# A fixed instruction order for the first mixer of a two-layer trunk, with two maps' logits on two row halves

## The chip, the cores and the metric

The kernel runs on one core of one Trainium2 chip. A core has five engines with queues of their own: TensorE (PE; its weight loads are listed apart as PEld), VectorE (DVE), ScalarE (ACT), GpSimd (POOL) and SyncE (SP, which only starts transfers). They share the on-chip memory SBUF; PE writes its products to the eight banks of PSUM, from where DVE and ACT fetch them. The metric is the device time of one execution in microseconds (us), the median of several runs.

## The reference

A trunk of two layers works on 512 tokens of 1024 features. In each layer a norm is followed by two mixers that share one output projection, then by sixteen experts of which a token uses two, then by a gated embedding. The change is in layer 0, whose mixers are A (differential attention, four heads) and B (a matrix memory, four heads). Mixer A, shortened:

```python
qa = rope(heads(qa, 8, 64)); ka = rope(heads(ka, 8, 64)); va = heads(va, 4, 128)
for each head n, each block of 128 queries:
    logits[m] = q[2n+m] @ k[2n+m].T / 8        # m = 0, 1: the two maps of a head, 64 features each
    logits[m] = where(key_chunk <= query_chunk, logits[m], -inf)
    probs[m]  = softmax(logits[m])
    out       = (probs[0] - lam * probs[1]) @ v[n]
out = rmsnorm(out, gain) * (1 - lam_init)
```

Mixer B takes q and k of its heads through a causal convolution of width 4 and a SiLU, multiplies decayed products of q and k with the values, normalizes, and gates the result. `concatenate([A, B]) @ w_out` is added to the residual `h`.

## The kernel before

All weights come as one stream of units of [128, 1024]; two units are one transfer of 1 MB on SP's queue. `unit` (L220) splits a unit into two float32r parts whose sum is the weight: ACT writes the upper part (`whi`, L193), DVE the rest (`wlo`, L194). A product of two split operands is three matmuls (`mm3`, L231 to L234). One head's q or k is `proj_f` (L260): one unit, 24 matmuls of 512 columns into one bank of the ring `m`. There are two rings of four PSUM banks, `m` and `w`.

Mixer A starts at L471. `rotated` (L473) projects q and k of a head, and ACT evicts them into `qk` (L477); four transfers on POOL's queue write a copy with the 32-row groups swapped (`sw`, L480); POOL multiplies `sw` with the sines (L481), DVE multiplies `qk` with the cosines (L482) and adds both (L483). Then come the four blocks of 128 queries, and block i sees 128 (i + 1) keys. For each of the two maps, `logits` multiplies 64 rows of q and k (L499: map 0 is on partitions 0 to 63, map 1 on 64 to 127), adds the mask by a product with the identity (L500, bfloat16), and calls `softmax_block`: maximum (L360), its negation (L361), exponential with a sum (L362), reciprocal (L363). L511 to L513 combine both maps, `put_T` turns the block (L369, L370), `pv` multiplies with the values (L383), and `mean_ln` (L330) with L517, L518 scales the result of a head. In it, ACT squares (L333) and splits (L334), DVE makes the lower part (L335), and PE sums both parts over the partitions (L338, L339).

Mixer B follows: `values(vb)` and the gates `og` are 192 matmuls, each head has two projections with `conv_silu` (L289), and `out_proj` (L344) multiplies the results of mixer A, 96 matmuls, and later those of B.

Nothing of this order is binding. The recording layer schedules all instructions of the mixers by priorities and estimated costs, so each engine's queue mixes several heads and stages. Within a queue every engine is in order. A tile of a ring is free again when its last reader is done.

Of the kernel before, what the change touches and what calls it, by code (L numbers as in the profile page):

```python
# [16 lines left out]
S = 512  # L17
DM = 1024
T = 4
# [9 lines left out]
# columns of the constants that follow from the shapes  # L29
# [4 lines left out]
# columns of the small parameters  # L34
# [17 lines left out]
# rooms that the units of a further block take in turn  # L52
# [14 lines left out]
def _layer_units(layer):  # L67
    """Order in which the units of [128, 1024] weights are used."""
    if layer == 0:
# [3 lines left out]
        u += [("T", 5, k) for k in range(4)] + [("T", 6, k) for k in range(4)]  # L73
        for n in range(NH):
            u += [("F", 3, n), ("F", 4, n)]
# [30 lines left out]
def tile_hybrid_trunk(ctx, tc, x, wst, gains, small, lam, rwt, cst, out, stop=None):  # L106
# [49 lines left out]
    def transposed(cx):  # L156
        """Room for transposed rows, in two parts."""
        xtp = cx.enter_context(pool_("xt", 1))
        xt[:] = [xtp.tile([128, KD, S], F32R, name="xt" + i) for i in "hl"]

    def banks(cx, **n):
        """Banks of PSUM for one part of the kernel: "m", and one or more rings for the rest."""
        W.psum = cx.enter_context(pool_("psum", 1, space=bass.MemoryType.PSUM))
        W.banks = n
        W.ring = "w"
# [13 lines left out]
    def load(src, eng=None, pool=None, c=None):  # L179
        """A chunk of two units."""  # L180
# [7 lines left out]
    def split(src, a=None, place=None):  # L188
        """Two parts of a unit."""
# [9 lines left out]
    def ahead(eng=None, pool=None):  # L199
        """Load the next chunk of the stream before its units are asked for."""  # L200
# [35 lines left out]
    def norm_scale(t, xn, r):  # L236
        """1 / sqrt(mean(h^2) + eps) of a tile's tokens; xn is room for the squares."""
# [42 lines left out]
    def values(v):  # L280
        """Values by token, [128, tile, 128] for each head."""
# [19 lines left out]
    def rows_split(r, rows):  # L301
        """Rows of four heads as two exact parts, on partitions 0 and 32."""
# [9 lines left out]
    def log_sigmoid_rows(r4, ps, r0, bias):  # L312
        """log(sigmoid(rows + bias)) at partitions 0 to 3, and a spare row."""
# [9 lines left out]
    def cols_of(c, rows):  # L323
        """Rows [4, 512] as columns [128, tile, head]."""
# [5 lines left out]
    def mean_ln(tmp, src, scale):  # L330
        """log(scale * sum over partitions of src^2 + eps), on every partition."""
# [12 lines left out]
    def out_proj(mix):  # L344
        m = len(mix)
        for nh in range(2):
# [10 lines left out]
    def softmax_block(p, ps, n):  # L357
        """exp(ps - max) and 1 / sum over the n keys of one block of queries."""
        nm = st.tile([128, 4], F32, name="nm", bufs=6)
        nc.vector.reduce_max(nm[:, 0:1], ps[:, :n], axis=AX.X)  # L360
        ts(nm[:, 1:2], nm[:, 0:1], -1.0, None, op0=OP.mult)  # L361
# [49 lines left out]
    banks(ctx, m=4, w=4)  # L411

    def even_mixer():
        with ExitStack() as cx:
# [31 lines left out]
            # gates of the mLSTM  # L446
# [17 lines left out]
            # rows of the results that no block may write  # L464
# [6 lines left out]
            # A  # L471
            mix = []
            def rotated():  # L473
                qk = mp.tile([128, 2, S], F32, name="qk")
                for i in range(2):
                    ps = proj_f(unit("F", 8))
                    act(qk[:, i, :], ps, AF.Copy, scale=0.125 if i == 0 else 1.0)  # L477
                sw = mp.tile([128, 2, S], F32, name="sw", bufs=1)
                for q in range(4):
                    nc.gpsimd.dma_start(out=sw[q * 32:(q + 1) * 32], in_=qk[(q ^ 1) * 32:(q ^ 1) * 32 + 32])  # L480
                nc.gpsimd.tensor_tensor(sw, sw, sinb, op=OP.mult)  # L481
                tt(qk, qk, cosb, op=OP.mult)  # L482
                tt(qk, qk, sw, op=OP.add)  # L483
                return qk

            qkn = rotated()
            for n in range(NH):
                qk = qkn
                if n + 1 < NH:
                    qkn = rotated()  # L490
                wt = mp.tile([128, 4, S], F32, name="wt", bufs=1)

                def logits(i):
                    nk = 128 * (i + 1)
                    pr = []
                    for m in range(2):
# [906 lines left out]
```

## Time and profile before

| what | value |
|---|---|
| three runs | 1488.6, 1483.21, 1483.45 us; median 1483.45 us |
| profiled execution, first to last instruction | 1487.2 us |
| PE busy in it | 1396.7 us (94%) |
| DVE busy | 1118.5 us (75%) |
| ACT busy | 916.9 us (62%) |
| POOL busy | 136.9 us (9%) |
| mean granted clock of TensorE | 0.974 |

The profiled execution is another one than the three runs, and of its own time the table has the span alone; the launch around the span is not part of it. Matmuls overlap in their pipeline, so a busy PE says only that there is something in it. How fast a stretch goes is read from the starts of its matmuls. The granted clock is 1.00 at full speed and 0.50 at half.

### The profile page before, as it was taken

The numbers are of one execution on the slowest core, as the hardware profiler recorded it, in microseconds if no ns is written. First come the engines' busy times: TensorE is split into PE (matmuls) and PEld (weight loads), VectorE is DVE, ScalarE is ACT, GpSimd is POOL, SyncE is SP. The second block draws the span as 40 slices with busy tenths as digits, with TensorE's granted clock in tenths as the row PEclk, the third lists the DMA queues.
The fourth block names the chain that finished last, engine by engine and source line by source line (L and its number), as shares of the span: only waits on it lengthen the run. The fifth ranks groups of instructions, "written<-read, shape, count | busy, mean of one in ns | idle before, by whom it ended". The sixth has DMA issues, their size and how long they took to land. (4 is left out here: it accounts for less than half of the span.)

```text
span 1487.2 us, 18591 instructions
## 1 busy us (share of the span) xinstructions
PE 1396.7 (94%) x6728; PEld 1096.0 (74%) x6728; DVE 1118.5 (75%) x1633; ACT 916.9 (62%) x1424; POOL 136.9 (9%) x143
## 2 busy tenths in 40 slices
PE   6999999969987999999999999999969989999996
PEld 4765677748865888877787887878648868888875
DVE  5466568679976999987776556575589979999875
ACT  4334566348865888885655536452448868888855
POOL 2121012010000000003011000100010000000030
PEclk9998999989999999999999999999989999999998
DMA  9331123478985999915431111111478989999261
GB/s 346 134 95 43 57 85 119 186 265 322 412 353 210 410 404 410 396 74 221 142 113 37 50 57 58 58 49 37 198 265 325 420 338 404 404 407 387 93 252 57
DMA packets 54652, 323.28 MB, mean 217 GB/s; under 512 B 6481, under 2 KB 6897, under 8 KB 23569
## 3 DMA queue, kind: packets, MB, share of 16 engines
q1 hardware_dynamic: 36576, 250.38, 43.7%
q0 software_dynamic: 12640, 52.16, 9.4%
q10 hardware_dynamic: 5328, 19.40, 3.3%
q8 instruction: 57, 0.93, 0.3%
q14 instruction: 51, 0.41, 0.1%
HBM read 292.55 MB, written 27.26 MB: 215 GB/s over the span
## 5 line engine op out<-in xcount | busy, mean ns | idle before, releaser
L194 DVE TENSOR_TENSOR wlo<-raw,whi 128x1024 fp32r<-128x1024 f32 x478 | 565.8, 1223 | 92.6 <-ACT whi L193 91.1
L193 ACT CAST whi<-raw 128x1024 fp32r<-128x1024 f32 x478 | 492.3, 1055 | 166.3 <-PE m L234 94.8
L232 PE MATMUL m<-whi,eh 128*128 128x512 f32 x528 | 213.4, 404 | 1.6 <-ACT whi L193 1.6
L233 PE MATMUL m<-wlo,eh 128*128 128x512 f32 x528 | 210.6, 399 | 1.5 <-DVE wlo L194 1.4
L234 PE MATMUL m<-whi,el 128*128 128x512 f32 x528 | 210.0, 398 | 0.0
L233 PE MATMUL m<-xtl,whi 128*128 128x512 f32 (+1 forms) x368 | 142.5, 388 | 0.8 <-DVE xtl L257 0.8
L234 PE MATMUL m<-xth,wlo 128*128 128x512 f32 (+1 forms) x368 | 142.9, 389 | 0.0
L232 PE MATMUL m<-xth,whi 128*128 128x512 f32 (+1 forms) x368 | 141.7, 386 | 0.5 <-ACT xth L256 0.5
L232 PE MATMUL m<-whi,xth 128*128 128x512 f32 x288 | 118.3, 412 | 2.7 <-ACT xth L256 1.2
L233 PEld LDWEIGHTS m<-wlo,eh 128*128 128x128 f32 x528 | 100.3, 190 | 25.6 <-DVE wlo L194 3.4
L232 PEld LDWEIGHTS m<-whi,eh 128*128 128x128 f32 x528 | 100.4, 190 | 25.1 <-ACT whi L193 2.1
L234 PE MATMUL m<-whi,xtl 128*128 128x512 f32 x288 | 117.1, 408 | 1.6 <-DVE xtl L194 1.1
L234 PEld LDWEIGHTS m<-whi,el 128*128 128x128 f32 x528 | 99.9, 189 | 24.3 <-DVE el L842 0.8
L233 PE MATMUL m<-wlo,xth 128*128 128x512 f32 x288 | 116.8, 406 | 0.5 <-DVE wlo L194 0.5
L232 PE MATMUL m<-whi,hh 128*128 128x512 f32 x256 | 102.9, 407 | 0.0
L233 PE MATMUL m<-wlo,hh 128*128 128x512 f32 x256 | 101.8, 399 | 0.3 <-DVE wlo L194 0.3
L234 PE MATMUL m<-whi,hl 128*128 128x512 f32 x256 | 102.0, 399 | 0.0
L233 PEld LDWEIGHTS m<-xtl,whi 128*128 128x128 f32 x368 | 70.6, 192 | 13.0 <-DVE xtl L257 1.0
L232 PEld LDWEIGHTS m<-xth,whi 128*128 128x128 f32 x368 | 70.5, 192 | 12.7 <-ACT xth L256 0.9
L234 PEld LDWEIGHTS m<-xth,wlo 128*128 128x128 f32 x368 | 70.5, 192 | 11.7 <-issue 0.7
L849 POOL DMA_INDIRECT xg<-xrow,toki x32 | 34.1, 1066 | 488.6 <-PE w L839 432.9
L841 ACT CAST eh<-w 128x512 fp32r<-128x512 f32 x82 | 46.9, 590 | 39.1 <-PE w L839 37.8
(427 smaller groups left out, 2307.0 us busy)
## 6 DMA issues: line engine op xcount, KB each, us to landing
raw<-in_wst_dram SPq DMA_DIRECT2D x226, 1024.0 KB, 7.8
raw<-in_wst_dram POOLq DMA_DIRECT2D x14, 1024.0 KB, 7.5
yrow<-y ACTq DMA_DIRECT2D x17, 512.0 KB, 8.6
yrow<-gbc ACTq DMA_DIRECT2D x14, 512.0 KB, 8.3
xrow<-raw POOLq DMA_DIRECT2D x8, 512.0 KB, 6.3
yrow<-tmp POOLq DMA_DIRECT2D x14, 256.0 KB, 9.8
h<-in_x_dram SPq DMA_DIRECT2D x4, 512.0 KB, 13.1
sw<-qk POOLq DMA_DIRECT2D x16, 128.0 KB, 2.8
```

Source lines behind the costliest of these rows:

```text
L193: nc.scalar.copy(hi, src)
L194: nc.vector.tensor_sub(lo, src, hi.bitcast(F32))
L232: mm(ps, l[0], r[0], start=start, stop=False)
L233: mm(ps, l[0], r[1], start=False, stop=False)
L234: mm(ps, l[1], r[0], start=False, stop=stop)
L841: W.turned = nc.scalar.copy(eh[o], ps)
L849: ins = nc.gpsimd.indirect_dma_start(out=xg, out_offset=None, in_=xrow, in_offset=bass.IndirectOffsetOnAxis(ap=idx, axis=0))
```

## The change

Mixer A is written in a fixed order for PE, DVE and ACT (`manual_schedule`; what stands outside of the block may still be placed between). Its parts:

- The two maps of a block have their products one after the other, then both masks; both maxima, then both exponentials; one reciprocal of both sums. The maximum is negated by the instruction that finds it, in mixer D of the other layer too.
- The projections run two heads ahead, in pieces of 6, 6, 12, 9 and 15 matmuls between the steps of a head. Heads "4" and "5" of this count are the first two of mixer B, so four units of the stream come earlier and the eight units of B's values and gates later. Room for four more halves of q and k comes from `og`, which is not yet in use.
- The product with the sines is on DVE, not on POOL.
- The maxima of blocks 0 and 1 of a head stand ahead of the scaling of the head before, whose steps (`squares`, `scale_of`, `scaled`, `finish`) are spread over the next head. Turned blocks go to ring `m`.
- In mixer B, `out_proj` of A's results is cut in halves, one ahead of head 2 and one ahead of head 3.

```diff
-        u += [("T", 5, k) for k in range(4)] + [("T", 6, k) for k in range(4)]
         for n in range(NH):
+            if n == 2:
+                u += [("T", 5, k) for k in range(4)] + [("T", 6, k) for k in range(4)]
             u += [("F", 3, n), ("F", 4, n)]
...
-        nc.vector.reduce_max(nm[:, 0:1], ps[:, :n], axis=AX.X)
-        ts(nm[:, 1:2], nm[:, 0:1], -1.0, None, op0=OP.mult)
+        nc.vector.reduce_max(nm[:, 1:2], ps[:, :n], axis=AX.X, negate=True)
...
+            def logits(n, i):
+                nk, qk = 128 * (i + 1), pairs[n]
+                lg[i] = [pw([128, S]) for _ in range(2)]
+                for m in range(2):
+                    r = slice(64 * m, 64 * m + 64)
+                    mm(lg[i][m][:, :nk], qk[r, 0, i * 128:(i + 1) * 128], qk[r, 1, :nk], start=True, stop=False)
+                for m in range(2):
+                    mm(lg[i][m][:, nk - 128:nk], identb, maskc, start=False, stop=True)
...
+            take(1, 1)
+            project(1, 0)
+            evict(1, 0)
+            project(1, 1)
+            rotate(0, 0, 1, 2)
+            evict(1, 1)
+            swap(1)
+            take(2, 0)
+            begin(0)
+            done = None
             for n in range(NH):
+                a = n + 2
+                wt = mp.tile([128, 4, S], F32, name="wt", bufs=1)
+                project(a, 0, 0, 2)
+                combine(0)
+                if done:
+                    squares(*done)
+                combine(1)
+                take(a, 1)
+                project(a, 0, 2, 4)
+                if done:
+                    done = scale_of(*done)
+                turn(wt, 0)
+                logits(n, 2)
+                exps(2)
+                if done:
+                    scaled(*done)
+                rotate(n + 1, 0, 1)
+                project(a, 0, 4)
+                evict(a, 0)
+                combine(2)
+                turn(wt, 1)
+                logits(n, 3)
+                exps(3)
+                rotate(n + 1, 2)
+                if done:
+                    mix.append(finish(xp, done[1]))
+                project(a, 1, 0, 3)
+                turn(wt, 2)
+                combine(3)
+                project(a, 1, 3)
+                if n + 1 < NH:
+                    take(a + 1, 0)
+                evict(a, 1)
+                swap(a)
+                turn(wt, 3)
+                if n + 1 < NH:
+                    begin(n + 1)
+                done = result(n, wt)
```

`begin(n)` is `logits` and `exps` of blocks 0 and 1; `take` splits a unit, `project` is its matmuls, `combine` is L511 to L513 with the reciprocal.

On PE, block 2 of the first head of mixer A before (`w` are banks, `qk` the rotated q and k, three digits tell tiles apart):

```order
L499 MATMUL w_626<-qk_440 128x384
L500 LDWEIGHTS identb_71
L500 MATMUL w_626<-maskc_72,identb_71 128x128
L499 MATMUL w_635<-qk_440 128x384
L500 LDWEIGHTS identb_71
L500 MATMUL w_635<-maskc_72,identb_71 128x128
```

and the same block in the changed kernel, where L517 is the product and L519 the mask:

```order
L517 MATMUL w_645<-qk_443 128x384
L517 MATMUL w_646<-qk_443 128x384
L519 LDWEIGHTS identb_71
L519 MATMUL w_645<-maskc_72,identb_71 128x128
L519 LDWEIGHTS identb_71
L519 MATMUL w_646<-maskc_72,identb_71 128x128
```

The product of map 1 now follows that of map 0 with nothing between them, and they write two banks.

On DVE, around the lower part of the squares of head 0's result (L335) before. `qk_711` is the pair of the head after the next:

```order
L512 TENSOR_SCALAR tmp_664<-tmp_664,c1_679 128x512
L513 SCALAR_TENSOR_TENSOR tmp_655<-tmp_655,nm_656,tmp_664 128x512
L194 TENSOR_TENSOR wlo_1341<-raw_1338,whi_1340 128x1024
L482 TENSOR_TENSOR qk_711<-qk_711,ce_208 128x1024
L335 TENSOR_TENSOR tmp_696<-tmp_694,tmp_695 128x512
```

and the same step (now L556) in the changed kernel:

```order
L526 TENSOR_REDUCE nma_757<-w_745 128x1
L526 TENSOR_REDUCE nma_757<-w_746 128x1
L526 TENSOR_REDUCE nma_764<-w_751 128x1
L526 TENSOR_REDUCE nma_764<-w_752 128x1
L534 RECIPROCAL nma_757<-nma_757 128x2
L535 TENSOR_TENSOR nma_757<-nma_757,lmb_213 128x1
L536 TENSOR_SCALAR tmp_759<-tmp_759,nma_757 128x128
L537 SCALAR_TENSOR_TENSOR tmp_758<-tmp_758,nma_757,tmp_759 128x128
L556 TENSOR_TENSOR tmp_778<-tmp_776,tmp_777 128x512
L534 RECIPROCAL nma_764<-nma_764 128x2
```

Four maxima of the next head and its first combination stand ahead of that step now, and the product with the cosines behind it.

POOL's queue in mixer A before, from the second head's swapping transfer (L480) to the fourth's:

```order
L480 DMA sw_574<-qk_511 32x1024 x4
L481 TENSOR_TENSOR sw_574<-sw_574,ce_208 128x1024
L480 DMA sw_774<-qk_711 32x1024 x4
L524 MEMSET v_1242 128x4
L481 TENSOR_TENSOR sw_774<-sw_774,ce_208 128x1024
L480 DMA sw_974<-qk_911 32x1024 x4
```

and all of mixer A in the changed kernel, where L500 is that transfer (L643 sets a column of B's values):

```order
L500 DMA sw_513<-qk_443 32x1024 x4
L500 DMA sw_579<-qk_444 32x1024 x4
L500 DMA sw_734<-og_442 32x1024 x4
L643 MEMSET v_1290 128x4
L500 DMA sw_913<-og_442 32x1024 x4
```

No product is left on POOL in mixer A. From head 3 of mixer B on, PE's rows stand in the order of before, up to the last head of layer 1's mixers.

## Rows read from the trace of the kernel before

**Rows 1.** The page: the span, and busy time of each engine.

```profile
span 1487.2 us, 18591 instructions
PE 1396.7 (94%) x6728; PEld 1096.0 (74%) x6728; DVE 1118.5 (75%) x1633; ACT 916.9 (62%) x1424; POOL 136.9 (9%) x143
```

**Rows 2.** Busy time by stretch: length, then each engine; PEclk is the granted clock.

```profile
49.50:113.76 64.26, 61.85 (x265) 44.85 (x263) 38.23 (x64) 21.96 (x41) 14.50 (x16) 1.00 0.31 99
113.76:124.00 10.24, 10.24 (x23) 6.32 (x24) 5.99 (x21) 3.65 (x11) 0.00 (x0) 0.50 0.00 0
124.00:216.20 92.20, 91.73 (x378) 62.16 (x376) 56.65 (x127) 51.03 (x109) 7.47 (x8) 1.00 0.21 71
```

**Rows 3.** Timeline of 109.6 to 113.9: start, duration, engine, line; idle before it.

```profile
109.69 3.41 POOL L481 TENSOR_TENSOR sw<-sw,ce 128x1024 f32<-128x1024 f32 x1 [1.35 <-DMA sw<-qk]
...
110.79 2.85 DVE L335 TENSOR_TENSOR tmp<-tmp 128x512 fp32r<-128x512 f32 x1
...
111.75 0.39 PE L234 MATMUL m<-whi,xtl 128*128 128x512 f32 x1
...
113.69 0.76 PE L339 MATMUL w<-tmp,oner 128*128 128x512 f32 x1 [1.56 <-DVE tmp L335]
```

**Rows 4.** The line L335: duration in ns, minimum, median, maximum of four.

```profile
L335 DVE TENSOR_TENSOR tmp<-tmp x4: 692/1270/2848, 110.8 to 186.1; 128x512 fp32r<-128x512 f32 x4
```

**Rows 5.** PE's timeline, logits of head 0, each block's first row and the next step.

```profile
86.77 0.48 PE L499 MATMUL w<-qk 64*128 64x128 f32 x2
...
87.93 0.70 PE L499 MATMUL w<-qk 64*128 64x256 f32 x2
...
89.38 0.48 PE L233 MATMUL m<-xtl,whi 128*128 128x512 f32 x1
...
92.48 0.91 PE L499 MATMUL w<-qk 64*128 64x384 f32 x2
...
94.39 0.39 PE L369 MATMUL w<-cs,tmp 128*128 128x128 f32 x2
94.71 1.12 PE L499 MATMUL w<-qk 64*128 64x512 f32 x2
95.76 0.23 PE L500 MATMUL w<-maskc,identb 128*128 128x128 bf16 x1
95.92 1.12 PE L499 MATMUL w<-qk 64*128 64x512 f32 x2
...
97.02 0.48 PE L233 MATMUL m<-xtl,whi 128*128 128x512 f32 x1
```

**Rows 6.** PE's timeline, product with the values of head 0, and what follows.

```profile
105.79 2.38 PE L383 MATMUL w<-wt,v 128*128 128x512 f32 x8
107.92 0.48 PE L234 MATMUL m<-whi,xtl 128*128 128x512 f32 x1
```

**Rows 7.** PE's timeline, first and last of 38 projection rows in one sequence.

```profile
77.82 0.40 PE L234 MATMUL m<-xth,wlo 128*128 128x512 f32 x1
...
86.46 0.39 PE L232 MATMUL m<-xth,whi 128*128 128x512 f32 x1
```

**Rows 8.** DVE by line, 78 to 200: count, busy us, mean ns, idle before.

```profile
L360 DVE TENSOR_REDUCE nm<-w 128x1 f32<-128x128 f32 (+3 forms) x32 | 15.5, 489 | 14.8 <-PE w L500 14.8
L194 DVE TENSOR_TENSOR wlo<-raw,whi 128x1024 fp32r<-128x1024 f32 x12 | 14.7, 1222 | 11.8 <-ACT whi L193 11.8
L513 DVE SCALAR_TENSOR_TENSOR tmp<-tmp,nm 128x128 f32<-128x128 f32 (+3 forms) x16 | 8.8, 549 | 0.3
L512 DVE TENSOR_SCALAR tmp<-tmp,c 128x128 f32<-128x128 f32 (+3 forms) x16 | 6.1, 381 | 0.3
...
L363 DVE RECIPROCAL nm<-nm 128x1 f32<-128x1 f32 x32 | 4.7, 156 | 2.6 <-ACT tmp L362 2.6
L361 DVE TENSOR_SCALAR nm<-nm 128x1 f32<-128x1 f32 x32 | 4.5, 148 | 0.3
```

**Rows 9.** PE's timeline near the end of layer 1's mixers.

```profile
1052.47 0.66 PE L375 MATMUL w<-cs,w 128*128 128x128 f32 x2 [1.57 <-DVE nm L361]
```

## What is predicted

> **What bounds the kernel now.** I first read the page for the share of each engine [rows 1]: PE has something in it for 94% of the span, DVE for 75%. That does not yet say that PE is the limit in layer 0's mixers, so I read the stretches of them with the granted clock [rows 2]. PE is busy for 61.85 of 64.26 us before 113.76, for all of the 10.24 us behind it, and for 91.73 of the next 92.20. The reader should see two things there: almost no idle time, and a clock of 0.50 in the 10.24 us. So mixer A is bound by what stands in PE's queue and by the clock, not by the latency of its softmax: the old order fills it already. What a new order can gain is work taken off PE, the stretch at half clock, and the one real wait.
>
> Where that wait comes from is in the timeline ahead of the slow stretch [rows 3]. POOL multiplies with the sines from 109.69 to 113.10. DVE's L335 starts at 110.79 and takes 2.85 us, though the same instruction takes 0.69 at best [rows 4], and ends with POOL's. PE's L339 needs it: idle for 1.56 us, from 112.1 to 113.7, and from 113.76 on the clock is 1.2 GHz instead of 2.4.
>
> **What PE loses in work.** In the timeline of head 0's logits a block, two maps with masks, takes 1.16, 1.45, 1.91 and 2.31 us for 128 to 512 keys, from its first row to the next step [rows 5]; together 6.83 us, times four heads 27.3. The trace shows each fp32 product as two instructions. What a full pass costs is seen in the product with the values: eight of them, two for each of 512, 384, 256 and 128 columns, in 107.92 - 105.79 = 2.13 us [rows 6], so one pass over 1280 columns takes 1.065 us, and over 512 columns 0.43. Of the 6.83 us of a head, four passes (two maps, two instructions) are 4.26. The other 2.57 are the masks and the changes between 64-row products and products on all rows, 0.64 a block.
>
> The changed order has one such change per block instead of two, since both products stand together: half of 0.64, less 0.06 for the second mask, which stays (128 columns at the pace of [rows 7]), is 0.26 a block, 1.03 a head, **4.1 us** in all. That holds even if the products run strictly one after the other. Beyond it, the two maps use different rows and different banks. Their overlap is not in this trace, so I bound it: nothing is saved, or, if both maps run side by side entirely, two of the four passes, 2.13 us a head, 8.5 in all. I take the middle, one pass of four, 4.3 us: the two instructions of map 0 use the same rows and must follow each other, so only the second of them and the first of map 1 are neighbours on different halves. Sum of this part: **-8.4**, bounds -4.1 and -12.6.
>
> The Trainium skill says the same of the neighbours: in "TensorE: Matmul & The Clock Gate", section "Part 3: Packing small matmuls", matmuls on different row groups run at once, some 4 ns apart, while starts stay in queue order. No run here shows it yet. By it the sum is the -8.4; by the rows alone, whose nearest case is the product after a mask, it could be -4.1. "TensorEngine Tiling (Array Packing)", section "Key Properties", says that a change of tiling mode drains the engine; the 0.64 us a block of overhead agree.
>
> **What the clock and the wait give back.** The 10.24 us at half speed hold work of 5.12 us [rows 2], and 1.56 us were idle [rows 3]. Their cause goes: the product with the sines is a DVE instruction now, and POOL computes nothing in mixer A. **-5.1 and -1.6**. Bounds: nothing, if the new order makes another wait of that length, and -6.7.
>
> The Trainium skill explains the 2.85 us: "SBUF — State Buffer", section "SBUF: two separate sides", says of the port pair that DVE and GpSimd share that it is an exclusive lock, held for a whole instruction, against DVE instructions with two SBUF inputs. The row agrees, since both ended together. By a shared bandwidth, the other reading, the sum would be the same.
>
> **What moves.** Four units of B's projections come into mixer A and eight units of values and gates leave it. PE's count of projection matmuls stays, at (86.46 - 77.82) / 37 = 0.2335 us each [rows 7]; their price is 0 because PE has no idle time to lend or to fill. If that cover were gone, 96 matmuls are 22 us, but they are only moved.
>
> DVE gets more. Per head from [rows 8]: maxima 15.5 / 4 = 3.9, splits of two units 2.4, L513 2.2, L512 1.5, one reciprocal and one small product a block 4 x (0.16 + 0.15) = 1.2, three rotations 3 x 1.22 = 3.7, and three passes over 512 columns at 0.69 [rows 4], 2.1. Together 17.0 us. Without the change it would be 1.2 less for the third rotation, and 1.8 more for eight negations (0.148) and four reciprocals (0.156). PE's head: 48 projections 11.2, logits 6.83 - 2.1 = 4.7, ten turned blocks of 128 columns at 0.83 ns a column (0.43 / 512, [rows 6]), 1.1, values 2.1, sums of two passes 0.8, so 19.9. DVE is at 85% of PE: it fits, but in a fixed order it must also come in time.
>
> I walked head 1 with these durations, in queue order. PE reaches the sums of head 0 at 2.8 us, their lower part is ready at 2.2; logits of block 2 at 3.7; maxima to 6.3, exponentials to 7.3, two rotations to 9.3, the combination of block 2 to 10.7, which PE's turn wants at 12.0; logits of block 3 end at 9.9, maxima at 11.9, the last combination at 15.9. PE wants that one at 15.8 for the last turn. A wait of some 0.2 us in each of four heads, 0.8. At the start, the split of unit (2, 0) stands behind an eviction on ACT. I take ACT's eviction and its half of the split at DVE's pace for the same tiles, 0.69 [rows 4] and 1.22 [rows 8], and DVE's half at 1.22: 3.1 us, against logits of two blocks in 1.16 + 1.45 - 0.6 [rows 5] and two products in 0.47: a wait of some 0.6, 0.5 to 0.8. In mixer B, head 3 follows head 2 after 48 projections where 96 stood; its chain over DVE and ACT takes about as long as PE's 17 us, so up to 0.5. Together **+2.0**, bounds 0.5 and 4.
>
> Mixer D loses 16 negations of 0.15 us on DVE. The one PE wait behind a negation, 1.57 us [rows 9], is for a combination that stands behind other DVE work in the changed order as well. I take 0; bounds: gone with its half clock, about -5, or 2 longer.
>
> **Sum.** -8.4 - 5.1 - 1.6 + 2.0 = -13.1 us. The experts that follow see the same PE order, so the gain is carried to the end. It is worked out in the profiled execution, whose span is 1487.2 us [rows 1], 3.75 above the median of the runs; I take the difference off the median: 1483.45 - 13.1 = **1470.4 us**, 0.9% faster. About 0.5%, 7.4 us, can be told from no change.
>
> **The rivals.**
> - *The halves do not run together.* Only 4.1 us of PE work go: -8.8, 1474.7 us. For it: the trace has no overlap of two fp32 products. Against: disjoint rows, two banks.
> - *They overlap entirely.* -12.6 - 6.7 + 2.0 = -17.3, 1466.1 us. Against: PE takes its queue in order, and the second map stands behind both instructions of the first.
> - *One new wait like the old one.* Some step that the walk has as ready comes 1.6 us late once, and PE falls to 1.2 GHz for another 10.24 us as in [rows 2]: +6.7, so -6.4, 1477.1 us. For it: the order is fixed, and three places have under 0.5 us to spare.
> - *DVE sets the pace, slower than before.* The place is the last combination of each head: its maxima wait for PE, and two rotations, a split and the scaling of the last head stand ahead of it on DVE. If it comes 1.6 us late in every head, each costs 1.6 + 5.1: 26.8 us, so +13.7, 1497.2 us. It decides from the point where DVE's share of a head passes some 18.5 instead of 17.0. Against: DVE is rid of POOL's product, which had doubled its instructions.
> - *It does nothing*, if the old order were bound by transfers; but [rows 2] show PE full.
>
> **How the numbers follow.** The forecast has 0.42; no overlap 0.18; full overlap 0.10; one new wait 0.20; slower 0.10. 1470.4 is the first case. The range reaches from 1462 (full overlap, few waits, and a part of mixer D's bound) to 1479 (one new wait with less overlap); it leaves out the slower case and the outermost parts. Faster by over 0.5%: the first three and a small part of the fourth, 0.73. Within 0.5%: the rest of the fourth, 0.17. Slower: 0.10.
>
> **What would show it.** The clock at 1.00 all through mixer A, DVE's squares at 0.69, no POOL product. A block of 512 keys in about 1.6 us from first row to next step: 2.05 would be no overlap, 1.2 full overlap. PE's waits below 1 us, the longest ahead of the first head's projection and the last turn. Mixer B's last two heads with no new wait. The forecast is wrong if a wait of over 1.5 us stands in any head, if the clock falls again, or if the gain of mixer A is missing at the end of layer 0.

## The result, and the profile after

The changed kernel takes 1470.95 us (median of 4 runs, 1465.68 to 1475.78) against 1486.03 us for the kernel before in the same runs (4 runs, 1483.21 to 1491.99): a ratio of 0.9895, 95% interval 0.987 to 0.992. Two later comparisons on other runs gave 1470.02 us, ratio 0.9877 (0.9856 to 0.9898), and 1470.88 us, ratio 0.989 (0.9868 to 0.9912). So it is faster by 1.0 to 1.2%, and the forecast of 1470.4 us holds. The working behind it holds less well, and that is what the rest is about.

First the page of the changed kernel, span and engines, which answers to [rows 1].

```profile
span 1474.0 us, 18496 instructions
PE 1381.5 (94%) x6728; PEld 1091.8 (74%) x6728; DVE 1112.3 (75%) x1573; ACT 918.9 (62%) x1428; POOL 127.7 (9%) x139
```

The shares have not moved: PE 94%, with 15.2 us less busy time. The next rows are busy time by stretch, with the columns of [rows 2]: mixer A from its first logits to its last product with the values; what lies between that and mixer B's first logits; mixer B's heads and the out projections, up to the first transpose of the router; and everything behind it.

```profile
73.39:150.46 77.07, 75.48 (x366) 52.41 (x366) 62.38 (x126) 49.03 (x116) 6.02 (x14) 1.00 0.32 103
150.46:208.51 58.05, 58.01 (x245) 45.20 (x244) 28.64 (x35) 31.01 (x51) 7.69 (x5) 1.00 0.21 75
208.51:287.37 78.86, 78.48 (x373) 60.98 (x373) 56.02 (x114) 37.38 (x102) 8.48 (x10) 1.00 0.47 179
287.37:1474.00 1186.63, 1109.64 (x5493) 886.66 (x5491) 931.24 (x1248) 773.36 (x1101) 94.47 (x86) 0.97 0.61 237
```

The granted clock is 1.00 in all of layer 0's mixers, where [rows 2] have 0.50 for 10.24 us. DVE is at 62.38 of 77.07 us in mixer A, 81%, and PE still has 98%. What PE waits for in layer 0's mixers is three lines of the waits (waiting line, releaser, us in total, times, longest):

```profile
PE m L542 <- ACT whi L194: 0.9, 1, 0.9
PE m L235 <- DVE wlo L195: 0.5, 1, 0.5
PE w L704 <- DVE tmp L700: 0.4, 1, 0.4
```

The first is the last turn of the last head, the second the split of unit (2, 0), both where the prediction looked for them; the third is in mixer B. The profile puts the first down to a split on ACT. In the third profile of the changed kernel, where the same wait is 0.87 us, the timelines of PEld, ACT and DVE say otherwise:

```profile
149.29 0.42 PEld L542 LDWEIGHTS m<-cs,tmp 128*128 128x128 f32 x4 [1.27 <-issue]
148.26 1.04 ACT L194 CAST whi<-raw 128x1024 fp32r<-128x1024 f32 x1 [1.01 <-PE m L234]
148.42 0.75 DVE L537 SCALAR_TENSOR_TENSOR tmp<-tmp,nma 128x512 f32<-128x512 f32 x1
```

The turn's weights began to load at 149.29, before ACT's split had ended at 149.30; what had ended at 149.17 is the last combination (L537). So PE waits for that combination, as the prediction had it.

Now a block of 512 keys, in PE's timeline, to be held against the two rows of L499 with their masks in [rows 5]:

```profile
120.74 0.38 PE L542 MATMUL m<-cs,tmp 128*128 128x128 f32 x2
121.05 1.13 PE L517 MATMUL w<-og 64*128 64x512 f32 x4
122.11 0.29 PE L519 MATMUL w<-maskc,identb 128*128 128x128 bf16 x2
122.21 0.47 PE L233 MATMUL m<-xth,whi 128*128 128x512 f32 x1
```

From its first row to the next step the block takes 122.21 - 121.05 = 1.16 us, where it took 2.31, and where 1.6 was forecast and 1.2 was named as the sign of full overlap. A window of the same timeline that holds only 121.50 to 121.58, while the first instructions still run, shows what stands side by side:

```profile
121.05 0.70 PE L517 MATMUL w<-og 64*128 64x512 f32 x2
```

Two instructions, of the two maps, both started at 121.05: the first pass of map 1 does not stand behind the second pass of map 0. That the two are not both of one map is settled by after_same_rows below, where the four stand on one half and start one after the other.

The table has, for each kernel that was run, where the router's first transpose stands in its trace (the end of layer 0's mixers), how long the logits of the four heads take in all, from each block's first row to the next step, and the time of the whole with its ratio to the kernel before in the same runs.

| kernel | router's first transpose, us | logits, us | median, us | ratio, 95% interval |
|---|---|---|---|---|
| before, two profiles | 307.17, 306.09 | 28.3 | 1486.03 | |
| changed, three profiles | 287.37, 288.49, 288.28 | 14.3 | 1470.95 | 0.9895 (0.987 to 0.992) |
| changed, logits apart | 298.62 | 27.3 | 1482.37 | 0.9967 (0.9948 to 0.9986) |
| changed, same rows | 294.04 | 22.5 | 1477.47 | 0.9934 (0.9911 to 0.9957) |
| changed, sines on GpSimd | 288.91 | 14.3 | 1472.36 | 0.9888 (0.9866 to 0.9909) |
| before, logits side by side | 301.94 | 19.7 | 1483.03 | 0.9981 (0.9961 to 1.0001) |
| before, sines on VectorE | 300.27 | 26.8 | 1482.22 | 0.9975 (0.9957 to 0.9994) |
| before, both edits | 291.67 | 17.9 | 1473.31 | 0.9924 (0.9898 to 0.995) |
| changed, trimmed, two profiles | 284.02, 283.68 | 12.7 | 1467.33, 1469.23 | 0.9876 (0.9852 to 0.9899), 0.9882 (0.986 to 0.9903) |
| changed, turned rows in the logits' ring | 287.32 | 14.6 | 1472.17 | 0.99 (0.9876 to 0.9924) |

The 28.3 us of the kernel before hold 1 us for the two maps of one block that fall into the stretch at half clock; at full clock it is the 27.3 of the prediction. The expectations that were written first count from a row 2.8 us behind the one in the table (290.2 and 310.0 us for 287.37 and 307.17); differences are the same by either.

### The profile page after: what moved, and what is told of

It is laid out like the page before. It is cut to its first block, busy times and chain, and to the rows that moved or that the text cites. A ratio compares the mean times of both kernels' runs of the same rounds, so it can differ in the third digit from the quotient of the medians.

```text
span 1474.0 us, 18496 instructions
## 1 busy us (share of the span) xinstructions
PE 1381.5 (94%) x6728; PEld 1091.8 (74%) x6728; DVE 1112.3 (75%) x1573; ACT 918.9 (62%) x1428; POOL 127.7 (9%) x139
## 5 line engine op out<-in xcount | busy, mean ns | idle before, releaser
L234 PEld LDWEIGHTS m<-xtl,whi 128*128 128x128 f32 x368 | 70.4, 191 | 12.6 <-DVE xtl L258 1.0
## 6 DMA issues: line engine op xcount, KB each, us to landing
h<-in_x_dram SPq DMA_DIRECT2D x4, 512.0 KB, 13.4
```

The costliest lines, as they stand in the source:

```text
L234: mm(ps, l[0], r[1], start=False, stop=False)
```

## The experiments

### Where the saving of the logits comes from

**after_apart** undoes the order of the logits alone.

```diff
                 for m in range(2):
                     r = slice(64 * m, 64 * m + 64)
                     mm(lg[i][m][:, :nk], qk[r, 0, i * 128:(i + 1) * 128], qk[r, 1, :nk], start=True, stop=False)
-                for m in range(2):
                     mm(lg[i][m][:, nk - 128:nk], identb, maskc, start=False, stop=True)
```

> The changed kernel with the old order of the logits alone: product and mask of map 0, then product and mask of map 1. Theory A, the saving in mixer A comes from the neighbourhood of the two products: each head's four blocks take 1.16, 1.45, 1.91 and 2.31 us again instead of 0.64, 0.75, 0.94 and 1.16, so 3.34 us a head and 13.4 us over the mixer, and the router's first transpose stands at 290.2 + 13.4 = 303.6 us; the whole is some 13 us slower than the changed kernel. Rival, part of the saving comes from the fixed order (the later maxima give the products room): the blocks take less than the old times, and the loss is nearer 4 to 8 us.

The logits take 27.3 us again, 13.0 more, so theory A holds on the blocks. The router comes 11.3 us later than in the first profile of the changed kernel, not 13.4: PE, slower now, waits nowhere over 0.2 us in mixer A, so the 1.4 us of waits above are paid back. The whole loses 12.4 us of the 16.7 that the changed kernel is ahead in the same runs (1482.37 and 1470.02 against 1486.76).

**after_same_rows** keeps that order and puts both maps on one half.

```diff
-                    r = slice(64 * m, 64 * m + 64)
+                    r = slice(0, 64)
```

> The changed kernel, with both maps' products on rows 0 to 63 (map 1's logits are those of map 0: this part of the computation is changed); order, lengths and masks stay. Theory A, the two products run at the same time because they stand on different row halves: with the same rows each head pays two more passes over 1280 columns, 2.13 us, so 8.5 us over the mixer, and a block of 512 keys takes about 2.0 us instead of 1.16; the rest of the saving, 4.9 us, stays. Rival, the saving comes from having one change between 64-row and full-row products in place of two, and the halves do not matter: the block of 512 keys stays at 1.16 us and the time does not move.

Its block of 512 keys in PE's timeline:

```profile
104.63 0.38 PE L542 MATMUL m<-cs,tmp 128*128 128x128 f32 x2
104.94 1.98 PE L517 MATMUL w<-qk 64*128 64x512 f32 x4
106.85 0.29 PE L519 MATMUL w<-maskc,identb 128*128 128x128 bf16 x2
106.95 0.48 PE L233 MATMUL m<-xth,whi 128*128 128x512 f32 x1
```

The same four instructions, in the same order, take 1.98 us instead of 1.13: on one half four passes follow each other (they start at 104.94, 105.47, 105.90 and 106.33), on two halves two by two run together. The logits take 22.5 us. That splits the saving: 27.3 - 22.5 = 4.8 us for one change fewer between 64-row and full-row products in each of 16 blocks, 0.30 us each (the same in a block of 384 keys, 1.88 - 1.58, as in one of 512, 2.31 - 2.01), and 22.5 - 14.3 = 8.2 us for the two halves. The rival, that the halves do not matter, is out.

### The wait behind GpSimd's product

**before_dve_sines** takes the product with the sines off GpSimd, and is otherwise the kernel before; the scheduler sets the order of the rest anew.

```diff
-                nc.gpsimd.tensor_tensor(sw, sw, sinb, op=OP.mult)
+                tt(sw, sw, sinb, op=OP.mult)
```

> The kernel before, with only the product with the sines moved from GpSimd to VectorE. Theory A, the prediction's: GpSimd's product made VectorE's subtraction late, TensorE waited 1.56 us and ran 10.24 us at half clock; without it 6.7 us go, and the router's first transpose stands at 300.5 us instead of 307.2. Rival, after the run with GpSimd's product in the fixed order, which cost nothing there: what matters is which instruction stands behind the blocked one, and with 4.9 us more on VectorE the old order makes another wait, so the router stays within 2 us of 307.

No wait of PE is left in its list from 60 to 216 us, the granted clock is 1.00 up to 315 us, and the router comes at 300.27: 6.9 us earlier than in the first profile of the kernel before, 5.8 earlier than in the second. In the median 3.9 us arrive (1482.22 against 1486.14 in the same runs). Theory A holds, in the old order.

**after_pool_sines** puts the product back on GpSimd in the new order.

```diff
-                        tt(sw[n], sw[n], sinb, op=OP.mult)
+                        nc.gpsimd.tensor_tensor(sw[n], sw[n], sinb, op=OP.mult)
```

> The changed kernel with the product with the sines back on GpSimd (as in the kernel before), all else in the fixed order. Theory A, as in the prediction: while GpSimd multiplies for some 3.4 us, VectorE's instructions on two operands in SBUF take up to 2.85 us instead of 0.7 to 1.2, the fixed order has under 0.5 us to spare at the last turn, so TensorE waits over 1 us in at least one head and falls to half clock there: 6.7 us for each such head, 7 to 20 us slower than the changed kernel in mixer A. Rival: VectorE is rid of 1.22 us a head and TensorE's wait is hidden by the projections ahead, so mixer A stays within 1 us of the changed kernel, and the gain of 6.7 us in clock and wait came from the order, not from moving the product.

The timelines of GpSimd and, below it, of VectorE in head 1:

```profile
101.24 2.37 POOL L507 TENSOR_TENSOR sw<-sw,ce 128x1024 f32<-128x1024 f32 x1 [5.75 <-DMA sw<-og]
```

```profile
100.67 0.74 DVE L569 SCALAR_TENSOR_TENSOR tmp<-m,sgain,tmp 128x512 f32<-128x512 f32 x1
101.33 3.37 DVE L505 TENSOR_TENSOR og<-og,ce 128x1024 f32<-128x1024 f32 x1
104.62 0.15 DVE L534 RECIPROCAL nma<-nma 128x2 f32<-128x2 f32 x1
```

The blocking of VectorE is there as before: its product with the cosines takes 3.37 us, not 1.22, and ends 104.70 - 103.61 = 1.09 us after GpSimd's, so it ran when the other was done. The end shows this in other heads too, whatever the start. Here is another head of the same run, GpSimd's product and VectorE's, whose end is 1.08 us behind again:

```profile
119.38 2.64 POOL L507 TENSOR_TENSOR sw<-sw,ce 128x1024 f32<-128x1024 f32 x1 [3.77 <-DMA sw<-og]
121.44 1.66 DVE L505 TENSOR_TENSOR og<-og,ce 128x1024 f32<-128x1024 f32 x1
```

In the kernel before, L335, which takes 0.69 us at best, ends 0.54 us behind GpSimd's product when it starts at 110.79 [rows 3], and 0.55 here:

```profile
136.67 2.38 POOL L481 TENSOR_TENSOR sw<-sw,ce 128x1024 f32<-128x1024 f32 x1
137.75 1.85 DVE L335 TENSOR_TENSOR tmp<-tmp 128x512 fp32r<-128x512 f32 x1 [1.60 <-ACT tmp L334]
```

It works the other way round too. GpSimd's product takes 2.38 us here, where it came first, and 3.41 in [rows 3], where VectorE's product with the cosines had started 0.04 us ahead of it:

```profile
109.65 1.22 DVE L482 TENSOR_TENSOR qk<-qk,ce 128x1024 f32<-128x1024 f32 x1 [3.19 <-DMA sw<-qk]
```

So GpSimd's product stood behind the product with the cosines there, and L335 behind GpSimd's.

But in the new order the victim is a rotation that nobody needs soon. In head 1 VectorE pays 2.15 us and is rid of a product of 1.22; PE's longest wait is 0.9 us, as in the changed kernel, the clock stays at 1.00, and the router stands at 288.91. The rival is right here: in the new order the place of the product does not matter. In the old order the instruction that stood behind GpSimd was L335, the subtraction that PE wanted at once [rows 3].

### Both edits without the new order

**before_pairs** has the logits side by side in the kernel before.

```diff
-                    pr = []
-                    for m in range(2):
-                        ps = pw([128, S])
+                    pp = [pw([128, S]) for _ in range(2)]
+                    for m in range(2):
                         r = slice(64 * m, 64 * m + 64)
-                        mm(ps[:, :nk], qk[r, 0, i * 128:(i + 1) * 128], qk[r, 1, :nk], start=True, stop=False)
-                        mm(ps[:, nk - 128:nk], identb, maskc, start=False, stop=True)
-                        pr.append(softmax_block(tmp(), ps, nk))
-                    return pr
+                        mm(pp[m][:, :nk], qk[r, 0, i * 128:(i + 1) * 128], qk[r, 1, :nk], start=True, stop=False)
+                    for m in range(2):
+                        mm(pp[m][:, nk - 128:nk], identb, maskc, start=False, stop=True)
+                    return [softmax_block(tmp(), pp[m], nk) for m in range(2)]
```

> The kernel before, with the two maps' logits side by side in each block (both products, then both masks) and nothing else edited; the scheduler then sets the order of the rest anew. From the run with the old order of the logits in the changed kernel, where the logits took 27.3 us for 14.3, theory A says that the neighbours carry most of the gain in any order: the logits of the four heads fall from 28.3 to about 14.5 us, and the router's first transpose from 307.2 to about 294 us; the whole is 0.9% faster than before. The wait behind the product with the sines and its half clock may stay or go with the new order. Rival: without the fixed order TensorE, now ahead of its softmax by 3.3 us a head, waits for VectorE, and under half of the 13 us arrive at the router.

Neither holds whole. The logits fall to 19.7 us only (1.1 of them at half clock, and 1.0 a wait that falls into a block), and the waits of mixer A grow:

```profile
PE w L339 <- DVE tmp L335: 3.5, 2, 2.5
PE w L369 <- DVE nm L363: 1.8, 1, 1.8
```

The wait behind GpSimd's product is 2.5 us instead of 1.56, and half clock follows for 10.24 us again, in which some of the blocks stand. Of 8.6 us saved on the logits 5.2 arrive at the router, and 3.1 in the median.

**before_both** has the two edits together.

> The kernel before, with both edits: logits side by side and the product with the sines on VectorE, in the scheduler's order, projections one head ahead. Theory A, the fixed order itself brings nothing: the router's first transpose comes at 287 to 289 us as in the changed kernel, and the whole is 1.2% faster than before. Rival, the fixed order pays for itself, since TensorE is now ahead of VectorE: waits of over 1 us, and a stretch at half clock with each, make the router 3 to 10 us later than in the changed kernel.

The router comes at 291.67 us, 15.5 ahead of the first profile of the kernel before and 3.2 to 4.3 behind the changed kernel. So theory A falls too, but no wait above 0.2 us is left in mixer A, so the rival's waits did not come. The 3.6 us lie in the logits, 17.9 for 14.3, and two things can be read there. The scheduler puts projections between the maps of the second block in three heads (two stretches of 0.67 us, for 0.75 in all). And the block of 512 keys takes 1.68 us in all four heads. Its timeline in one head, on PE and on ScalarE:

```profile
139.87 0.39 PE L369 MATMUL w<-cs,tmp 128*128 128x128 f32 x2
140.19 1.65 PE L498 MATMUL w<-qk 64*128 64x512 f32 x4
141.78 0.28 PE L500 MATMUL w<-maskc,identb 128*128 128x128 bf16 x2
```

```profile
140.30 0.37 ACT L370 COPY wt<-w 128x256 f32<-128x256 f32 x1 [1.02 <-PE w L369]
```

and the part of PE's timeline from 140.1 to 140.6 us alone:

```profile
140.19 0.69 PE L498 MATMUL w<-qk 64*128 64x512 f32 x1
```

Only one of the four runs until 140.6. The second map's product starts at 140.72, 0.05 us after ScalarE's copy of the turned rows has ended at 140.67, and so it is in each head. The profile names that copy as the releaser of its weights:

```profile
140.72 0.29 PEld L498 LDWEIGHTS w<-qk 64*128 64x128 f32 x2 [0.24 <-ACT wt L370]
```

It is three passes instead of two: the case that the prediction took for the rule.

**after_turn_w** asks whether the ring of the turned rows is the cause.

```diff
             def turn(wt, i):
-                ps = pm([128, 4, 128])
+                ps = pw([128, 4, 128])
```

> The changed kernel, with the turned rows in the ring of four banks that the logits use (as in the kernel before), instead of the ring of the projections. In the run of both edits in the old order, the block of 512 keys took 1.68 us, not 1.16: the second map's product starts 0.05 us after ScalarE's copy of the turned rows ends. Theory A, the bank is the reason: the second product of the block waits for the copy out of the bank it takes, so here too the blocks of 512 keys, and perhaps those of 384, take about 0.5 us more, 2 to 4 us over the mixer, and the router's first transpose comes at 290.5 to 292.5 us. Rival, the scheduler's order was the reason and the bank is not: the blocks stay at 0.94 and 1.16 us.

Theory A falls in this form: the blocks of 384 and 512 keys stay at 0.94 and 1.16 us, only the first two blocks of a head take 1.49 to 1.55 us together instead of 1.40, and the router stands at 287.32. With the turned rows in that ring, but the steps in the new order, the second product of a block does not come to stand behind the copy. Which bank it gets in the old order, and through what, was not tried further.

### What happens behind the router

**after_again** and **after_third** are the changed kernel, **before_again** the kernel before, all without an edit.

> The changed kernel once more, with more rounds. Its first profile is 19.8 us ahead of the kernel before at the end of layer 0's mixers (first transpose of the router at 290.2 for 310.0 us), and only 13.2 us at the end of the span: 2.8 us are lost in the wait of TensorE for an expert at 1205 us (6.95 us for 4.2), and about 4 us in stretches at half clock behind waits that both kernels have (17.07, 17.07 and 10.24 us for 13.65, 13.65 and 3.41). Theory A, these losses come and go from one execution to the next and have nothing to do with the change: layer 0 repeats within 0.5 us (router's first transpose at 290), while the stretches at half clock behind the routers and the wait for the expert come out with other lengths; the median lies between 1465 and 1475 us. Theory B, the change causes them (its shift puts the waits at another place against the weights' stream): the same lengths of 17, 17 and 10 us again, and the same 6.95 us.

> The changed kernel a third time, beside the trimmed one on the same chip. Theory: the logits take 14.3 us and the router's first transpose comes within 0.6 us of 288; what follows the router differs by several us from one execution to the next, as in the two profiles so far (1186.6 and 1185.8 us from there to the end of the span, where the kernel before has 1180.0 and the run of both edits 1177.7). Rival, the change itself lengthens what follows the router: again 1185 us or more.

> The kernel before once more, for its profile. In the profiles, the changed kernel is 18.7 to 19.8 us ahead at the router, but its median time is only about 16 us ahead; every kernel that gains at the router gives back 2 to 5 us by this comparison. Theory A, the first profile of the kernel before shows a wait that does not come in every execution: TensorE's 1.56 us behind GpSimd's product, or the 10.24 us at half clock, are missing this time, and the router's first transpose stands at about 300.5 to 306 us instead of 307.2. Theory B, the wait is there in each execution (router at 307 within 0.6 us), and the difference lies behind the router: 1177 to 1183 us from there to the end in the kernel before, against 1184.6 to 1186.6 in three profiles of the changed one.

Layer 0 repeats within 1.1 us, a little worse than expected, in both kernels: 287.37, 288.49 and 288.28; 307.17 and 306.09. The wait behind GpSimd's product is there a second time, 1.68 us, with 6.83 us at half clock, so it belongs to the kernel and theory A of the last expectation falls. From the router to the end it is 1180.0 and 1178.9 us in the kernel before, and 1186.6, 1185.8 and 1184.6 in the changed one. The wait for an expert, 6.95 us in the first profile, is 4.4 and 4.3 in the others: that one was chance. The rest goes with the stretches at half clock between the router and the output: read from the clock's record, they add up to 58.0 us in both profiles of the kernel before and to 71.7, 75.1 and 75.1 us in the changed one, behind the same waits in either. What PE does there is the same, as the rows of that stretch say, here of the second profile of the kernel before; the one for the changed kernel is the last row of the stretches above.

```profile
306.09:1485.00 1178.91, 1106.64 (x5493) 885.53 (x5491) 932.22 (x1264) 772.54 (x1101) 93.81 (x86) 0.97 0.61 238
```

The trimmed kernel below shows that one program has both lengths: 68.3 us at half clock and 1185.0 us from the router to the end in its first profile, 58.0 and 1178.3 in its second:

```profile
284.02:1469.00 1184.98, 1109.96 (x5493) 887.19 (x5491) 930.89 (x1248) 773.32 (x1101) 95.35 (x86) 0.97 0.61 237
```

```profile
283.68:1462.00 1178.32, 1104.94 (x5493) 884.46 (x5491) 930.44 (x1248) 772.71 (x1101) 94.75 (x86) 0.97 0.61 238
```

The same count of instructions is busy 5 us longer in the one than in the other. So it is not the change alone that sets these lengths, and other edits say the same: before_pairs, in the old order, has 75.1 us at half clock and 1184.5 from the router to the end, and after_apart, in the new one, 54.6 and 1180.3. Whether the change makes the longer ones likelier can be estimated from the granted clock of every execution on record: 2 x (1 - clock) x span is its time at half clock (79.6 us for the first profile of the changed kernel, whose own record adds up to 78.5). The mean is 72.0 us over 16 executions of the changed kernel and 74.9 over 68 of the kernel before. The difference, 2.9 us with a 95% interval of -1.3 to 7.2, is less than the 6.83 or 10.24 us that left mixer A. So it is likely, but not clear of the noise, that 4 to 7 us at half clock came back behind the router, 2 to 3.5 us of time; by what, stays open. The three profiled executions of the changed kernel are each the slowest of their series (1475.78, 1476.05 and 1474.68 us), so the profiles overstate this loss. The medians say that some 3 us of what is won at the router do not arrive: 15.1 to 16.7 us of 17.6 to 19.8.

### A trimmed order

**after_trimmed** moves three things in the new order.

```diff
             def begin(n):
-                for i in range(2):
-                    logits(n, i)
+                logits(n, 0, 1)
...
             rotate(0, 0, 1, 2)
+            take(2, 0)
             evict(1, 1)
             swap(1)
-            take(2, 0)
...
-                if done:
-                    mix.append(finish(xp, done[1]))
                 project(a, 1, 0, 3)
                 turn(wt, 2)
                 combine(3)
+                if done:
+                    mix.append(finish(xp, done[1]))
```

logits(n, 0, 1) issues the products of all its blocks first and then their masks.

> The changed kernel with three small edits of the order: the four products of a head's first two blocks side by side and then their four masks (one change between 64-row and full-row products less in each head, 0.3 us each: the first two blocks take 1.1 us instead of 1.40), the split of unit (2, 0) ahead of ScalarE's eviction of (1, 1) (its wait of 0.5 us goes), and the split of the finished head behind the last combination instead of ahead of it (the wait of 0.9 us at the last turn goes). Theory A: TensorE is still the bound, so all three arrive, 2.6 us in mixer A, the router's first transpose at about 285.5 us; the whole moves by 0.2%, which the runs can hardly tell. Rival: the maxima of the first block come later behind four products, a turn waits for them, and the sum is nothing.

> The trimmed order once more, beside the changed kernel on the same chip. Theory: 3 to 4 us ahead of it at the router (284 to 285 us), as in the first run (logits 12.7 us for 14.3, no wait above 0.5 us in mixer A); the median is 1465 to 1470 us, 0 to 0.4% under the changed kernel's. Rival: at the end of the run the two cannot be told apart.

The first two blocks of a head, in its timeline:

```profile
108.38 0.93 PE L518 MATMUL w<-og 64*128 64x128 f32 x8
109.24 0.40 PE L521 MATMUL w<-maskc,identb 128*128 128x128 bf16 x4
109.47 2.38 PE L551 MATMUL m<-wt,v 128*128 128x512 f32 x8
```

They take 1.09 us instead of 1.40, the logits 12.7 us in all, and no wait is left in mixer A, in both profiles. The router comes at 284.02 and 283.68, 3.4 to 4.8 us ahead of the changed kernel's three. In the whole it is 1467.33 us in its first comparison, and 1469.23 against the changed kernel's 1470.88 in the second: ratios to the kernel before of 0.9876 and 0.9882, against 0.9877 and 0.989. It is the fastest of all at the router, and at the end it cannot be told from the changed kernel.

## Why the prediction was right, and where it was not

**What bounds the kernel.** Right: PE's queue and the clock. Every edit that changed PE's work in mixer A moved the router by about that work, less the waits that came or went with it: 11.3 of 13.0 us in after_apart, 6.7 of 8.2 in after_same_rows, and in before_pairs 5.2 of 8.6, where waits took the place of the rest.

**The row halves, -8.4 us: the step that failed.** Measured are 27.3 - 14.3 = -13.0, a little beyond the bound of -12.6. The part for the changes between products was sized well, 4.8 for 4.1. The part for the overlap was 8.2 for 4.3, because of one sentence: that the two instructions of map 0 must follow each other, so that only the second of them and the first of map 1 are neighbours on different halves. In the trace both first passes start together and both second passes behind them. The middle case exists, 1.68 us for 512 keys where "about 1.6" was forecast, but in the old order, where the second product was late by one pass. The rival *they overlap entirely* was given 0.10 and against it stood that same sentence; at the router it is the one that came. The sentence from the Trainium skill beside the sum ("TensorE: Matmul & The Clock Gate", "Part 3: Packing small matmuls") has matmuls on different row groups running at once and starts in queue order. The row at 121.05 agrees with the first. The middle value follows from the second only if both instructions of map 0 stand ahead of map 1 in the queue; no view shows how the four stand there, and they did not start in that order.

**Clock and wait, -6.7 us.** The size is right: -6.9 and -5.8 by before_dve_sines against two profiles. The cause is right in the old order only. In the new order it is enough that another instruction stands behind GpSimd's product. One row was misread: L335 and GpSimd's product did not end together, L335 ended 0.54 us later. That it ends 0.54 or 0.55 us later whatever its start, and VectorE's longer product 1.08 or 1.09, fits a lock, the first of the prediction's two readings, and not a shared bandwidth.

**New waits, +2.0 us.** 1.4 in the first profile (0.5 at the start, forecast 0.5 to 0.8; 0.9 at the last turn). In the other two a further 0.6 and 0.9 us stand at a turn: 2.0 and 2.3. The last turn was forecast with 0.2 in each of four heads, 0.8 in all; it came in one or two, with 0.6 to 0.9 each. Mixer B has no new wait.

**What moves.** The projections cost nothing, as taken. Two heads ahead as against one brought nothing that can be seen: before_both, one head ahead, has no wait in mixer A either. DVE was forecast at 85% of PE in a head and is at 83% in mixer A (62.38 of 75.48 us). Mixer D's wait behind the last head is still there (1.6 us at L375), so 0 was right.

**The sum.** With the measured terms, the first pair of profiles has -13.0 - 6.7 - 0.9 + 1.4 = -19.2 at the router, and -19.8 was measured; over all profiles it is -17.6 to -19.8. The 0.9 are two smaller waits of the kernel before (0.5 us ahead of L369, 0.4 ahead of L339) that are gone too and that the prediction, with its "one real wait", did not count. The forecast was -13.1, and *the gain is carried to the end* was its second weak step: 13.2 us were left at the end of the first pair of profiles, 15.1 to 16.7 in the medians. So that 1470.4 us met 1470.95 is in part luck. The saving at the router was 4.5 to 6.7 us larger than forecast, and some 3 us of it did not arrive, so that in the runs of the result it is 15.1, 2.0 more than forecast. And the kernel before took 1486.03 us in these runs, 2.6 more than the 1483.45 from which the forecast was taken off. The 2.0 and the 2.6 cancel to 0.6.

**The rivals.** *The halves do not run together* is out by after_same_rows. *One new wait* and *DVE sets the pace* did not come: no wait reached 1 us, and no half clock fell into mixer A.

## What to carry to other kernels

Two products of 64 rows on the two row halves cost as much as one when nothing stands between them and both have their banks (1.06 us from the first start to the mask for 512 columns, where one alone had 1.05 in [rows 5]); a mask or a projection between them costs the pair, so issue the products of a block together, and of two blocks if the banks allow it. When one engine blocks another, look at which instruction stands behind the blocked one before moving work: the same blocking cost about 6 us at the router where PE waited for the next result, and nothing where it did not. And a gain of a per cent in one stage should be read in that stage's trace, because what follows can differ by 6 to 7 us from one execution of one program to the next.

## What the runs showed of the hardware

- An fp32 product of 64 rows shows as two instructions. Of two such products side by side on different halves the first instructions start together, and then the second ones: 1.13 us for four instructions over 512 columns, against 1.98 on one half.
- One change from 64-row to full-row products and back costs 0.30 us: 4.8 us over 16 blocks, the same in blocks of 384 and 512 keys, and 1.40 - 1.09 again for the one that the trimmed order takes away.
- VectorE's products with two operands in SBUF and GpSimd's product ran one after the other, whichever came first. VectorE's of 1.22 us ended 1.08 or 1.09 us behind GpSimd's in three heads, with durations of 1.66, 2.49 and 3.37 us, and the one of 0.69 us ended 0.55 and 0.54 us behind, with 1.85 and 2.85 us. GpSimd's took 2.38 us when it came first, and 3.41 when a product on VectorE had started 0.04 us before.
- The length of a wait did not say by itself whether half clock came. Waits of 0.9 us in mixer A had none behind them in four profiles, and neither had one of 1.81 us at 93.7 us in before_pairs; those of 1.56, 1.68 and 2.5 us that end at 113.7 to 114.3 us had 10.24, 6.83 and 10.24 us at 1.2 GHz. The clock fell 0.07 and 1.6 us after the end of the first two, and 0.9 us before the end of the third.
